# Later additions to x in both ffn_out stages, and three small edits in the attention of a macaron block on one core

## The chip, the core and the metric

The kernel runs on one core of a Trainium2 chip. A core has a matrix engine (TensorE, PE in the profile), a vector engine (VectorE, DVE), a scalar engine (ScalarE, ACT), a general engine (GpSimd, POOL) and a queue engine that issues most transfers (SyncE, SP). Each engine works through its own list of instructions in order; they meet only at semaphores. An instruction that must wait therefore holds up all that stand behind it on its engine, whatever these need.

The metric is the device time of one launch in microseconds (us), the median of several executions.

## The reference

One block: half a SwiGLU feed-forward, a causal mixer, and another half feed-forward. The depth is one, so the mixer is the stick-breaking attention. x has 1024 rows and 1024 columns, the feed-forward is 2816 wide, and there are 16 heads of 64.

```python
x = x + 0.5 * swiglu(rms_norm(x, g1), w1_in, w1_out)
x = x + stick_breaking_attention(rms_norm(x, gm), w_qkv, gq, gk, w_o)
x = x + 0.5 * swiglu(rms_norm(x, g2), w2_in, w2_out)

def swiglu(xn, w_in, w_out):
    gate, up = split(xn @ w_in, 2)
    return (silu(gate) * up) @ w_out

# stick breaking, for each head, t the later frame, s < t:
z = q[t] . k[s] / sqrt(64)            # q, k after rms_norm with gains
A[t, s] = sigmoid(z[t, s]) * prod over s < j < t of (1 - sigmoid(z[t, j]))
o[t] = sum over s of A[t, s] * v[s];  out = o @ w_o
```

Everything is float32.

## The kernel before

**Precision.** Each operand of a large matmul is kept as two parts, hi and lo, in the fast float format (fp32r). `split` makes them: ACT copies the number into the format (hi, L182), and DVE or POOL subtracts that from the number (lo, L183). `mm3` (L272) then issues three matmuls for each pair of tiles: hi by hi (L279), hi by lo of the weights (L280), lo by hi (L281).

**Order of the stages.** Feed-forward 1 (`first_pair`, `ffn_in`, `ffn_out`), attention with its output projection, feed-forward 2 (the same three functions). So `ffn_out` runs twice: as the first stage spoken of below, with `w1_out`, and as the last stage of the kernel, with `w2_out`.

**`ffn_out`.** The product h @ w_out is made by a Strassen-like scheme of seven products over halves, in the order of the table `SEVEN`: 5, 1, 4, 3, 7, 2, 6. Products accumulate in four PSUM banks each (`ma` or `mb`, one for every block of 128 rows, t = 0 to 3). Each product runs over six chunks of the inner dimension: chunks 0 to 4 with two steps of 128, chunk 5 with one. `operands` (L520) prepares a chunk: the sum of two weight tiles on DVE where the product needs one (L524), then hi of the weights on ACT and their lo on POOL, hi of h on ACT and its lo on DVE, or on POOL for the chunks in `ON_POOL_H` (1, 3 and 5 of product 6). In a trace `rp<-raw` is a part of the weights and `rp<-rh` one of h. The rooms for these parts hold four chunks and are used in turn.

When a product is complete, `result` (L566) adds its banks, times plus or minus one half, to x in SBUF, with one instruction on DVE for each block and half (L570). Product 2 goes to two places, so it has eight such additions. Product 6, the last one, does chunks 0 to 2 for all four blocks, and then chunks 3, 4, 5 block by block, so that each block's addition can follow at once.

**`held`.** Without it, product 2's eight additions are issued as soon as product 2 ends. With `held=n` the scale of these additions is not a constant but a tile, `signs`, which is first written from the lo part of h of chunk n of product 6 (L576) and then set to the constants (L536). The numbers are the same, but the additions can't come ahead of that lo part in DVE's list. Before the change the first stage has `held=2`; the last stage has none.

**What follows the additions in the first stage.** `at` (L665) hangs the work for the attention's input on them: squares of x on ACT (L217), the row norms on DVE (L242 writes the normalised rows, `xs`), stores of x to DRAM on SP (L672). The first weights of the attention come on the same queue (L733), are made hi on ACT (L739) and lo on POOL (L742), as wqh and wql.

**Attention.** Eight head pairs, in an interleaved plan. `weights_of` (L718) puts tiny writes, "holds", into the room of the next weights, so that ACT can't make these weights ahead of a given point: L738 writes 128x2 elements made from a given tile, on POOL or on DVE. `scores` (L829) makes a piece of w: two sigmoids on ACT (L853), a running product on DVE (L855, om), and their product on POOL (L862). `values` (L866) turns w by a transpose on PE (L884), splits it (th on ACT, tl on DVE), and multiplies with v (L902). `out_weights` (L1027) loads and splits w_o for the projection while the last pairs still run; its rooms are wa, wb, wc and so on.

Of the kernel before, what the change touches and what calls it, by code (L numbers as in the profile page):

```python
# [9 lines left out]
F32 = mybir.dt.float32  # L10
# [3 lines left out]
ALU = mybir.AluOpType  # L14
# [3 lines left out]
P = 128  # L18
# [88 lines left out]
def macaron_kernel(ctx, tc, x, g1, w1_in, w1_out, gm, w_qkv, gq, gk, w_o, g2, w2_in, w2_out, out):  # L107
# [64 lines left out]
    make_identity(nc, ident)  # L172
    xh = cpool.tile([P, KD, T], F32R, name="xh")
    xl = cpool.tile([P, KD, T], F32R, name="xl")
    above = cpool.tile([P, 96], F32, name="above")
    pool_e.memset(below, 0.0)
    pool_e.memset(above, 0.0)
    x_keep = [dram.tile([T, D], F32, name=f"x_keep{i}") for i in range(2)]
# [439 lines left out]
    with pools(*RAWS) as pr:  # L618
        ops = {}
        right = ExitStack()  # L620
        tl = mixed(right.enter_context(pools(*MIXED, side="right")))
        with banks("ps1"), pools(*STREAM) as pa:
            with pools("x") as px, pools("xs", "hs", side="right") as pl:
                rows_of = {}

                def load_x(tbs):
                    for tb in tbs:
                        rows_of[tb] = px["x"].tile([P, D], F32, name="x", bufs=NT)
                        sp.dma_start(rows_of[tb], x[rows(tb), :])

                def normed(tbs):
                    pending.extend(norm(pl, lambda tb, h: rows_of[tb][:, HALVES[h]], tbs, gain))

                def turn_rows(tbs):
                    while pending:
                        pending.pop(0)("kb", tl)
                    if tbs:
                        normed(tbs)

                load_x(ORDER[:2])  # L640
                gain = load_gain(pl, g1)
                ahead = [stream(pr, w1_in, 0, 0)]
                load_x(ORDER[2:4])
                ahead.append(stream(pr, w1_in, 0, 1))
                load_x(ORDER[4:])
                for tb in ORDER[:2]:
                    normed((tb,))

                us = first_weights(pa | pr, ahead, pending[1].args[0][:, D - 1 :])
                turn_rows(ORDER[2:4])  # L650
                at = {(0, 3): 4, (1, 1): 6, (2, 1): 8}
                hb = first_pair(
                    pa | pr, us, {w: lambda i=i: turn_rows(ORDER[i : i + 2]) for w, i in at.items()}
                )
            with pools(*SPLIT) as pt:
                ffn_in(pa | pr | pt, w1_in, keep, tl, hb, right, lambda: early(pr, w1_out, keep, ops))
        late = []
        norms = ExitStack()
        pn = norms.enter_context(pools("xs", "hs", side="right"))
        with banks("ps2"), pools(*SECOND) as pl:  # L660
            lay_banks()
            gain_m = load_gain(pn, gm)
            half = pn["xs"].tile([P, 4, 2], F32, name="half", bufs=1)

            def at(x_sb, m, where, ops):  # L665
                def row(tb, h):
                    return x_sb[h][:, tb, :]

                def store(tbs, hs):
                    for tb in tbs:  # L670
                        for h in hs:
                            sp.dma_start(x_keep[0][rows(tb), HALVES[h]], row(tb, h))  # L672

                def turn_rows(bk, n):
                    for _ in range(n):
                        pending.pop(0)(bk)

                if (m, where) == (7, "end"):
                    pending.extend(norm(pn, row, (4, 5), gain_m))
                    store((4, 5, 6, 7), (0, 1))  # L680
                elif (m, where) == (2, 2):
                    turn_rows("ma", 2)
                elif (m, where) == (2, 3):
                    late.append(rates(pn, row, (6, 7)))
                elif (m, where) == (6, 0):

                    there = ops[2][1][1][:, 0, 0:1].bitcast(F32)
                    pending.extend(norm(pn, row, (6, 7), gain_m, r=late.pop(), behind=there))
                elif (m, where) == (2, "end"):
                    squares(pn, row, range(4), half, (0,))  # L690
                    store(range(4), (0,))
                elif m == 6 and str(where).startswith("block"):
                    t = int(where[-1])
                    turn_rows("mb", (2, 0, 0, 1)[t])
                    squares(pn, row, (t,), half[:, t : t + 1], (1,))
                    late.append(lambda: pending.extend(norm(pn, row, (t,), gain_m, half[:, t : t + 1])))
                    if t < 3:
                        late.pop()()
                    store((t,), (1,))

            ffn_out(pl | pr, w1_out, keep, x, ops, at, held=2)

    on_banks = ExitStack()
    on_banks.enter_context(banks("psa"))
# [3 lines left out]
    with ExitStack() as stack:  # L708
# [9 lines left out]
        def weights_of(p, state, behind):  # L718

            wh, wl = state["wq"] = {}, {}

            def step(n, k):
                if k % 4 == 0:
                    wq = pl[f"wq{(2 * p + k // 4) % 4}"]
                    state["h"], state["l"] = (wq.tile([P, 4, 3 * P], F32R, name=f"wq{n}", bufs=1) for n in "hl")
                h_, l_ = state["h"], state["l"]
                raw = pl["raw_qkv"].tile([P, 2, 3, P], F32, name="raw_qkv")  # L730
                src = w_qkv[k * P : (k + 2) * P, :].rearrange("(k p) (a c) -> p k a c", p=P, a=3)
                for i in range(2):
                    sp.dma_start(raw[:, i], src[:, i, :, p * P : (p + 1) * P])  # L733
                ks = slice(k % 4, k % 4 + 2)
                raw = raw.rearrange("p k a c -> p k (a c)")
                for engine, to, f in behind[n]:
                    there = f().to_broadcast([P, 2])
                    engine.tensor_tensor((h_, l_)[to][:, ks, 0], there, there, op=ALU.mult)  # L738
                act.activation(h_[:, ks], raw, AF.Copy)  # L739
                for i in range(2):  # L740
                    k_ = k % 4 + i
                    pool_e.tensor_tensor(l_[:, k_, :], raw[:, i, :], h_[:, k_, :].bitcast(F32), op=ALU.subtract)  # L742
                    wh[k + i], wl[k + i] = h_[:, k % 4 + i, :], l_[:, k % 4 + i, :]

            return [partial(step, i // 2, k) for i, k in enumerate((4, 6, 0, 2) if p == 0 else (0, 2, 4, 6))]
# [83 lines left out]
        def scores(state, hd, half):  # L829
# [3 lines left out]
            def step(tb, kb):  # L833
                L = T - tb * P
                if kb == half:
                    t = pl["w"].tile([P, T - tb % 4 * P], F32, name=f"w{hd}{tb % 4}", bufs=1)

                    om = t[:, L : 2 * L] if half else pl["om"].tile([P, T], F32, name="om")
                    state["om"], w[tb] = om, t[:, :L]
                om, wt = state["om"], w[tb]  # L840
                q = state["q", hd, half][:, (tb % 4) * P : (tb % 4 + 1) * P]
                s0 = max(tb * P, kb * NHALF)
                n = (kb + 1) * NHALF - s0
                c0 = s0 - tb * P
                off = P if n == P else 0
                z = bank("bz")
                keys = slice(s0 - off - kb * NHALF, NHALF)
                for i in range(2):
                    pe.matmul(z[:, : off + n], q, state["k", hd, kb][i][:, keys], start=i == 0, stop=i == 1)  # L849

                z = z[:, off : off + n]
                for to, sign in ((wt[:, c0 : c0 + n], 0), (z, 1)):
                    act.activation(to, z, AF.Sigmoid, scale=state["f", half][:, sign, tb % 4, hd : hd + 1])  # L853
                least = first[:, P : P + 1].to_broadcast([P, n]) if c0 else first[:, :n]
                dve.tensor_tensor_scan(  # L855
                    om[:, c0 : c0 + n], z, least, initial=om[:, c0 - 1 : c0] if c0 else 0.0,
                    op0=ALU.mult, op1=ALU.max,
                )
                if c0 == 0:
                    pool_e.memset(wt[:, 0:1], 0.0)  # L860
                c1 = max(c0, 1)
                pool_e.tensor_tensor(wt[:, c1 : c0 + n], wt[:, c1 : c0 + n], om[:, c1 - 1 : c0 + n - 1], op=ALU.mult)  # L862

            return [partial(step, tb, kb) for tb in range(half * 4, half * 4 + 4) for kb in range(half, 2)]

# [157 lines left out]
    with pools(*PROJECTION) as pl:  # L1023
# [3 lines left out]
        def out_weights(c, k, rooms):  # L1027
# [7 lines left out]
            if c is HALVES[0] and k < 6:  # L1035

                there = seen[:, k // 2 : k // 2 + 1] if k < 4 else wo[-1][1][:, 0:1].bitcast(F32)
                pool_e.tensor_tensor((l_ if k < 4 else h_)[:, 0:1], there, there, op=ALU.mult)
            split(raw, h_, l_, lane(f"wo{k // 2}") if c is HALVES[0] else dve)
            return [(h_[:, s], l_[:, s]) for s in HALVES]  # L1040

        def project(tb, ks, h, tags):
# [48 lines left out]
    with banks("ps4"), pools(*SECOND) as pl:  # L1091
# [11 lines left out]
                for h in hs:  # L1103
                    sp.dma_start(out[rows(tb), HALVES[h]], x_sb[h][:, tb, :])

        ffn_out(pl | pr, w2_out, keep, x_keep[1], ops, at)
    after.close()


# [37 lines left out]
```

## Time and profile before

| | us |
|---|---|
| median of 3 runs | 1952.72 |
| lowest, highest | 1952.14, 1958.2 |
| the profiled execution | 1957.07 |
| span of its trace | 1955.3 |
| POOL busy | 1089.5 |
| DVE busy | 1265.6 |

The profile is one execution. A row of a timeline gives the start and the length of an instruction in us, its engine, its line in the program, the operation, and what it writes and reads (out<-in); in brackets stands how long the engine was idle before it, and what ended that. A list of waits gives, for an engine, which line waited for which line of which engine: total, times, longest. The chain that ended last is followed back from the last instruction of the kernel. A granted clock of 1.00 is TensorE's full speed.

### The profile page before, as it was taken

To read this page: it belongs to the slowest core of one execution; us is meant where nothing else is said; L and a number is where in the kernel's file an instruction comes from. 1 tells how busy PE (TensorE), PEld (TensorE's weight loads), DVE (VectorE), ACT (ScalarE), POOL (GpSimd) and SP (SyncE) were. 2 spreads that over 40 slices of the span, in tenths; PEclk is the share of its full clock that TensorE was granted. 3 is DMA by queue.
4 is the path that set the end of the run, shared out by engine and by line. 5 is a ranking of instruction groups with operands and counts; after the bars stand their busy time and mean duration, and the time that the engine had idled before them with its cause. 6 is when DMAs were issued, how large, how long until landed. Compare 5 with 4: busy or idle time off the path is not lost. (4 is left out here: it accounts for less than half of the span.)

```text
span 1955.3 us, 27335 instructions
## 1 busy us (share of the span) xinstructions
PE 1910.4 (98%) x9656; PEld 1638.2 (84%) x9656; DVE 1265.6 (65%) x1839; ACT 986.2 (50%) x1802; POOL 1089.5 (56%) x963
## 2 busy tenths in 40 slices
PE   7999999999999899999999999999999999999998
PEld 7978888888888798898989897789888888888886
DVE  7855545535766957877787878475555545557644
ACT  6533433434335467877787777344433443434331
POOL 3667666656455446555655664114667667655554
PEclk9999999999999999999999999999999999999999
DMA  6223223338996311011111144511323223369973
GB/s 210 85 88 126 101 92 114 107 113 284 343 325 231 124 34 44 31 46 45 36 34 46 55 130 151 194 55 44 130 86 124 96 99 105 117 231 345 325 251 128
DMA packets 168505, 260.26 MB, mean 133 GB/s; under 512 B 11568, under 2 KB 81200, under 8 KB 168368
## 3 DMA queue, kind: packets, MB, share of 16 engines
q1 hardware_dynamic: 168368, 258.52, 38.7%
q8 instruction: 75, 1.23, 0.3%
q14 instruction: 62, 0.51, 0.1%
HBM read 198.18 MB, written 60.29 MB: 132 GB/s over the span
## 5 line engine op out<-in xcount | busy, mean ns | idle before, releaser
L183 POOL TENSOR_TENSOR rp<-raw,rp 128x1024 fp32r<-128x1024 f32 x84 | 209.4, 2498 | 190.6 <-ACT rp L182 172.8
L183 POOL TENSOR_TENSOR u<-sf,u 128x512 fp32r<-128x512 f32 x160 | 225.9, 1414 | 151.1 <-ACT u L182 147.2
L183 POOL TENSOR_TENSOR u<-raw,u 128x512 fp32r<-128x512 f32 x136 | 195.8, 1444 | 164.7 <-ACT u L182 163.5
L182 ACT ACTIVATE u<-sf 128x512 fp32r<-128x512 f32 x160 | 100.7, 630 | 215.1 <-PE kb L280 86.7
L862 POOL TENSOR_TENSOR w<-w,om 128x512 f32<-128x512 f32 (+4 forms) x128 | 140.9, 1105 | 115.0 <-DVE om L855 88.8
L398 DVE TENSOR_TENSOR h<-h 128x512 f32<-128x512 f32 x110 | 135.4, 1235 | 85.7 <-POOL h L502 85.0
L279 PE MATMUL bq<-wqh,xh 128*128 128x384 f32 x512 | 174.7, 341 | 1.9 <-DVE vst L776 1.9
L182 ACT ACTIVATE rp<-rh 128x1024 fp32r<-128x1024 f32 (+1 forms) x78 | 76.4, 984 | 190.9 <-PE mb L280 62.0
L281 PE MATMUL bq<-wqh,xl 128*128 128x384 f32 x512 | 172.2, 336 | 0.0
L280 PE MATMUL bq<-wql,xh 128*128 128x384 f32 x512 | 172.1, 336 | 0.0
L279 PE MATMUL ka<-xh,u 128*128 128x512 f32 (+1 forms) x448 | 162.1, 362 | 1.8 <-ACT s L450 1.5
L280 PE MATMUL ka<-xl,u 128*128 128x512 f32 (+1 forms) x448 | 161.8, 361 | 0.0
L281 PE MATMUL ka<-xh,u 128*128 128x512 f32 (+1 forms) x448 | 161.6, 361 | 0.0
L182 ACT ACTIVATE u<-raw 128x512 fp32r<-128x512 f32 x136 | 85.0, 632 | 149.4 <-PE ka L280 101.3
L524 DVE TENSOR_TENSOR raw<-raw 128x1024 f32<-128x1024 f32 (+1 forms) x60 | 94.0, 1569 | 98.2 <-DMA raw<-w_out 92.4
L280 PE MATMUL ma<-rp 128*128 128x512 f32 x352 | 137.7, 391 | 4.4 <-POOL rp L183 4.4
L281 PE MATMUL ma<-rp 128*128 128x512 f32 x352 | 137.9, 392 | 3.3 <-DVE rp L183 3.3
L279 PE MATMUL ma<-rp 128*128 128x512 f32 x352 | 137.7, 391 | 0.0
L853 ACT ACTIVATE w<-bz,f 128x512 f32<-128x512 f32 (+2 forms) x192 | 112.3, 585 | 40.5 <-PE bz L849 39.4
L502 POOL TENSOR_TENSOR h<-h,g 128x512 f32<-128x512 f32 x80 | 112.9, 1411 | 35.2 <-DVE h L454 33.4
L427 DVE TENSOR_TENSOR sf<-raw 128x512 f32<-128x512 f32 x80 | 81.2, 1015 | 78.0 <-POOL u L183 78.0
L183 DVE TENSOR_TENSOR rp<-rh,rp 128x1024 fp32r<-128x1024 f32 (+1 forms) x70 | 108.4, 1567 | 22.4 <-ACT rp L182 19.7
(276 smaller groups left out, 5552.7 us busy)
## 6 DMA issues: line engine op xcount, KB each, us to landing
raw<-w_out SPq DMA_DIRECT2D x120, 512.0 KB, 5.6
raw<-w_in SPq DMA_DIRECT2D x88, 512.0 KB, 3.6
k<-h SPq DMA_DIRECT2D x154, 256.0 KB, 2.1
rh<-k SPq DMA_DIRECT2D x64, 512.0 KB, 6.2
raw_qkv<-w_qkv SPq DMA_DIRECT2D x64, 192.0 KB, 2.9
x_keep<-x SPq DMA_DIRECT2D x32, 256.0 KB, 3.5
x<-x_keep SPq DMA_DIRECT2D x32, 256.0 KB, 5.3
raw<-w_out SPq DMA_DIRECT2D x24, 256.0 KB, 4.3
```

Source lines behind the costliest of these rows:

```text
L182: act.activation(hi, raw, AF.Copy)
L183: (engine or dve).tensor_tensor(lo, raw, hi.bitcast(F32), op=ALU.subtract)
L279: pe.matmul(dst, ah, bh, start=start and i == 0, stop=False, skip_group_check=onto)
L280: pe.matmul(dst, ah, bl, start=False, stop=False, skip_group_check=onto)
L281: pe.matmul(dst, al, bh, start=False, stop=stop and i == n - 1, skip_group_check=onto)
L398: dve.tensor_tensor(src, hb[of[0]], hb[of[1]], op=getattr(ALU, of[2]))
L427: dve.tensor_tensor(f[n], x, y, op=op)
L502: pool_e.tensor_tensor(h, h, gs[k], op=ALU.mult)
L524: dve.tensor_tensor(w[0], w[0], w[1], op=getattr(ALU, W_OF[m][2]))
L853: act.activation(to, z, AF.Sigmoid, scale=state["f", half][:, sign, tb % 4, hd : hd + 1])
L862: pool_e.tensor_tensor(wt[:, c1 : c0 + n], wt[:, c1 : c0 + n], om[:, c1 - 1 : c0 + n - 1], op=ALU.mult)
```

## The change

Four edits. First, both calls of `ffn_out` pass `held=4`: the first stage had 2, the last stage none. `above`, a scratch tile, gives up eight columns for the second `signs` tile. Second, the holds on DVE (L738) are a TENSOR_SCALAR of one source rather than a TENSOR_TENSOR of the same source twice; their places stay. Third, the very last piece of w is multiplied on DVE and not on POOL. Fourth, in `out_weights` the lo part of one pair of weight tiles (k = 6 of the first half, wc on DVE) is written in two pieces of 128x512.

```diff
-    above = cpool.tile([P, 96], F32, name="above")
+    above = cpool.tile([P, 88], F32, name="above")
...
-            ffn_out(pl | pr, w1_out, keep, x, ops, at, held=2)
+            ffn_out(pl | pr, w1_out, keep, x, ops, at, held=4)
...
                     there = f().to_broadcast([P, 2])
-                    engine.tensor_tensor((h_, l_)[to][:, ks, 0], there, there, op=ALU.mult)
+                    if engine is dve:
+                        dve.tensor_scalar((h_, l_)[to][:, ks, 0], there, 1.0, None, op0=ALU.mult)
+                    else:
+                        engine.tensor_tensor((h_, l_)[to][:, ks, 0], there, there, op=ALU.mult)
...
-                pool_e.tensor_tensor(wt[:, c1 : c0 + n], wt[:, c1 : c0 + n], om[:, c1 - 1 : c0 + n - 1], op=ALU.mult)
+
+                last = state is states[NP - 1] and (hd, half, tb, kb) == (1, 0, 3, 1)
+                by = dve if last else pool_e
+                by.tensor_tensor(wt[:, c1 : c0 + n], wt[:, c1 : c0 + n], om[:, c1 - 1 : c0 + n - 1], op=ALU.mult)
...
-            split(raw, h_, l_, lane(f"wo{k // 2}") if c is HALVES[0] else dve)
+
+            act.activation(h_, raw, AF.Copy)
+            by = lane(f"wo{k // 2}") if c is HALVES[0] else dve
+            for s in HALVES if (c, k) == (HALVES[0], 6) else (slice(0, D),):
+                by.tensor_tensor(l_[:, s], raw[:, s], h_[:, s].bitcast(F32), op=ALU.subtract)
...
-        ffn_out(pl | pr, w2_out, keep, x_keep[1], ops, at)
+        ffn_out(pl | pr, w2_out, keep, x_keep[1], ops, at, held=4)
```

The order on the engines is set by a scheduler from the program, so `held` moves more than the additions. DVE in the first stage, from the addition of the weights of chunks 3 and 4 of product 6 (the first row) to the first addition to x (the last row), as a difference:

```order
 L524 TENSOR_TENSOR raw<-raw 128x1024 x2
 L183 TENSOR_TENSOR rp<-rh,rp 128x1024
+L240 TENSOR_SCALAR xs<-rp 128x1 x2
+L242 SCALAR_TENSOR_TENSOR xs<-x_4341,rs_y,gain 128x512
+L242 SCALAR_TENSOR_TENSOR xs<-x_4340,rs_y,gain 128x512 x2
+L524 TENSOR_TENSOR raw<-raw 128x512
+L183 TENSOR_TENSOR rp<-rh,rp 128x1024
 L576 TENSOR_SCALAR signs<-rp 128x2
-L240 TENSOR_SCALAR xs<-rp 128x1 x2
 L536 MEMSET signs 128x1 x2
-L242 SCALAR_TENSOR_TENSOR xs<-x_4340,rs_y,gain 128x512
 L570 SCALAR_TENSOR_TENSOR x_4340<-mb_5525,signs,x_4340 128x512
```

The two L183 are the lo parts of h of chunk 2 and chunk 4. Ahead of the additions there now stand three L242, the sum of chunk 5's weights (L524) and the lo part of chunk 4, which were among or behind the additions before; the eight additions are now together, with nothing between them.

ACT at the same place, before and then with the change, from chunk 3's parts to the hi part of the first weights of the attention. `rp` are parts of product 6, and `hs,half` are the squares, each of which waits for an addition to x:

```order
L182 ACTIVATE rp<-rh 128x1024
L182 ACTIVATE rp<-raw 128x1024
L217 ACTIVATE hs,half<-x_4340 128x512 x2
L182 ACTIVATE rp<-rh 128x1024
L182 ACTIVATE rp<-raw 128x1024
L217 ACTIVATE hs,half<-x_4340 128x512 x2
L182 ACTIVATE rp<-rh 128x512
L182 ACTIVATE rp<-raw 128x512
L739 ACTIVATE wqh<-raw_qkv 128x768 x2
```

```order
L182 ACTIVATE rp<-rh 128x1024
L182 ACTIVATE rp<-raw 128x1024
L182 ACTIVATE rp<-rh 128x1024
L182 ACTIVATE rp<-raw 128x1024
L217 ACTIVATE hs,half<-x_4340 128x512 x2
L182 ACTIVATE rp<-rh 128x512
L182 ACTIVATE rp<-raw 128x512
L217 ACTIVATE hs,half<-x_4340 128x512
L742 ACTIVATE wqh<-raw_qkv 128x768
L217 ACTIVATE hs,half<-x_4340 128x512
L742 ACTIVATE wqh<-raw_qkv 128x768
```

Chunk 4's two hi parts moved ahead of all squares; chunk 5's (128x512) stand behind two squares rather than four. (L742 of the changed kernel is L739 of the one before.)

DVE in the last stage, before (from the last two additions of product 2 to the first of product 6) and then with the change (from the sums of the weights of chunks 3 and 4 to the first two additions of product 2):

```order
L570 SCALAR_TENSOR_TENSOR x_17887<-mb_19044,x_17887 128x512
L570 SCALAR_TENSOR_TENSOR x_17888<-mb_19044,x_17888 128x512
L183 TENSOR_TENSOR rp<-rh,rp 128x1024
L524 TENSOR_TENSOR raw<-raw 128x512
L183 TENSOR_TENSOR rp<-rh,rp 128x1024
L570 SCALAR_TENSOR_TENSOR x_17888<-ma_19261,x_17888 128x512
```

```order
L524 TENSOR_TENSOR raw<-raw 128x1024 x2
L183 TENSOR_TENSOR rp<-rh,rp 128x1024
L524 TENSOR_TENSOR raw<-raw 128x512
L183 TENSOR_TENSOR rp<-rh,rp 128x1024
L576 TENSOR_SCALAR signs<-rp 128x2
L536 MEMSET signs 128x1 x2
L570 SCALAR_TENSOR_TENSOR x_17888<-mb_19042,signs,x_17888 128x512
L570 SCALAR_TENSOR_TENSOR x_17889<-mb_19042,signs,x_17889 128x512
```

The eight additions went from ahead of the two lo parts (chunk 2, chunk 4) and of the sum of chunk 5's weights to behind them.

Of the other lists: on SP in the first stage there were four stores of x and then eight loads of the attention's weights; now load and store alternate four times, a load first, and four loads follow. In the last stage the first store to the output moved behind the last load of w2_out. On PE one transpose (the w that DVE now makes) moved behind four other instructions. On DVE that multiply stands behind L908 and ahead of the next tl; the two pieces of wc follow each other at once.

## The prediction

> **What bounds the kernel now.** I read the page first, then PE's list of waits, then the chain of work that ended last, then the timeline at the places where these point.
>
> ```profile
> PE 1910.4 (98%) x9656; PEld 1638.2 (84%) x9656; DVE 1265.6 (65%) x1839; ACT 986.2 (50%) x1802; POOL 1089.5 (56%) x963
> ```
>
> PE is busy for 98% of the span of 1955.3 us, and the change takes no matmul away. So only time in which PE stands still, or runs below its pace, can be won. The list of PE's waits (total, times, longest) says where:
>
> ```profile
> PE bo L902 <- DVE tl L183: 7.7, 14, 1.2
> PE bt L884 <- POOL w L860: 4.7, 8, 0.6
> PE ma L280 <- POOL rp L183: 4.4, 2, 2.7
> PE ma L281 <- DVE rp L183: 3.3, 1, 3.3
> ```
>
> The last two rows are the sixth product of the two ffn_out stages, the place that `held` touches: twice in the first stage (4.4 us), once in the last one (3.3 us). The first row is spread over the attention. The chain that ended last comes out of the last stage:
>
> ```profile
> 1925.69 3.56 DVE x L570 x6
> ...
> 1929.80 1.22 DVE rp L183
> ...
> 1951.56 0.69 DVE x L570
> ```
>
> PE's end hangs there on one subtraction on DVE, the lo part of the h of chunk 2 (hl below), and that stands behind additions to x.
>
> **The last stage** (`held` from none to 4). First PE's timeline there, and from the table by windows the row behind the wait (length; busy time of PE, PEld, DVE, ACT, POOL; then the granted clock):
>
> ```profile
> 1927.15 0.39 PE L279 MATMUL ma<-rp 128*128 128x512 f32 x1
> 1927.38 0.39 PE L280 MATMUL ma<-rp 128*128 128x512 f32 x1
> 1931.06 0.79 PE L281 MATMUL ma<-rp 128*128 128x512 f32 x1 [3.30 <-DVE rp L183]
> ...
> 1934.82 0.39 PE L281 MATMUL ma<-rp 128*128 128x512 f32 x1
> 1931.00:1934.90 3.90, 3.84 (x10) 3.10 (x11) 1.75 (x3) 0.63 (x1) 1.47 (x1) 0.56 0.00 0
> ```
>
> PE's normal pace is 0.23 a step (1927.15 to 1927.38). From 1927.38 to 1934.82 there are 10 steps in 7.44 us, where 2.3 would do. So 5.1 us are lost: 3.4 by the wait, and 1.7 because the clock stood at 0.56 in the next 3.9 us (0.44 x 3.9). Now DVE and POOL:
>
> ```profile
> 1925.01 4.86 DVE L570 SCALAR_TENSOR_TENSOR x<-mb,x 128x512 f32<-128x512 f32 x8
> ...
> 1930.93 0.68 DVE L524 TENSOR_TENSOR raw<-raw 128x512 f32<-128x512 f32 x1
> 1931.53 1.21 DVE L183 TENSOR_TENSOR rp<-rh,rp 128x1024 fp32r<-128x1024 f32 x1
> 1926.32 2.38 POOL L183 TENSOR_TENSOR rp<-raw,rp 128x1024 fp32r<-128x1024 f32 x1 [2.31 <-ACT rp L182]
> ```
>
> After the change hl of chunk 2 starts at 1925.1, where the eight additions (4.86) started, and with its 1.21 is done by 1926.3; PE wants it at 1927.6. The addition of chunk 5's weights (0.68) and hl of chunk 4 (1.21) follow. A POOL subtraction beside them can stretch both (the same shape takes 3.42 at 643.01, below), so hl of chunk 4 ends between 1928.2 and 1931.2. PE wants it when the 24 steps of chunk 2 and seven more are done, at 1927.15 + 31 x 0.23 = 1934.3. The lo part of chunk 5's weights needs ACT and some 1.5 us of POOL behind the 0.68, so it is there by 1932.7 at the latest; PE wants it four to five steps later than hl of chunk 4. Then come `signs`, two memsets and the eight additions, done by about 1937. Block 0's addition waits behind them, which costs nothing: the one that ends the kernel is at 1951.56. On SP the first store to `out` goes behind the last load, and no one waits for it. Term: **-5.1 us**. If an execution has the wait without the slow clock, it is -3.4.
>
> Of such a clock the Trainium skill says ("TensorE: Matmul & The Clock Gate", Part 1) that an idle window of about 3.4 us halves it, that this window runs freely, and that the count of slow matmuls varies between runs. The trace agrees on the rate (the row of 0.56); whether other executions have it no row shows, and by that rule the term may lie at either of the two values above.
>
> **The first stage** (`held` from 2 to 4). PE, then ACT, DVE and POOL, which stand in each other's way:
>
> ```profile
> 656.10 0.50 PE L280 MATMUL ma<-rp 128*128 128x512 f32 x1 [2.69 <-POOL rp L183]
> ...
> 659.47 0.50 PE L280 MATMUL ma<-rp 128*128 128x512 f32 x1 [1.72 <-POOL rp L183]
> 641.50 1.06 ACT L182 ACTIVATE rp<-raw 128x1024 fp32r<-128x1024 f32 x1 [5.12 <-DVE raw L524]
> 648.17 0.63 ACT L217 ACTIVATE hs<-x 128x512 f32<-128x512 f32 x1 [5.61 <-DVE x L570]
> 643.01 3.42 DVE L183 TENSOR_TENSOR rp<-rh,rp 128x1024 fp32r<-128x1024 f32 x1
> ...
> 646.73 0.75 DVE L242 SCALAR_TENSOR_TENSOR xs<-x,rs_y,gain 128x512 f32<-128x512 f32 x1
> 647.39 1.40 DVE L570 SCALAR_TENSOR_TENSOR x<-mb,signs,x 128x512 f32<-128x512 f32 x2
> 642.64 2.71 POOL L183 TENSOR_TENSOR rp<-raw,rp 128x1024 fp32r<-128x1024 f32 x1 [2.32 <-ACT rp L182]
> 652.85 3.19 POOL L183 TENSOR_TENSOR rp<-raw,rp 128x1024 fp32r<-128x1024 f32 x1 [7.50 <-ACT rp L182]
> 656.00 1.75 POOL L183 TENSOR_TENSOR rp<-rh,rp 128x512 fp32r<-128x512 f32 x1
> 657.71 1.71 POOL L183 TENSOR_TENSOR rp<-raw,rp 128x512 fp32r<-128x512 f32 x1
> ```
>
> PE waits 2.69 us for POOL's lo of chunk 4's weights and 1.72 for that of chunk 5. Both are late because ACT sat 5.61 us in front of a square (L217) that waits for an addition, with the hi parts of both chunks behind it. After the change chunk 4's two hi parts stand ahead of the squares: ACT does them from 642.6 to 644.7 (1.06 each), POOL its lo from 645.35 to about 648.5 (3.19), and PE, which wants it at 656.10 - 2.69 = 653.4, waits no more. Chunk 5's hi parts still stand behind two squares, which wait for additions 1 and 3, and those are now later. DVE does hl of chunk 2 until 646.4, three L242 of 0.66 to 0.75 which POOL blocks until 648.5 (to 650.6), L524 (0.68), hl of chunk 4 (1.21), `signs` and memsets (0.3); so the additions start at about 652.7. The third ends at 654.8 (0.7 each), its square at 655.5, ACT's two parts of 0.6 at 656.7, and POOL's hl and then lo of chunk 5, short of the 1.7 that they take under contention, at about 659.0. PE gets there at 653.4 + (659.47 - 1.72 - 656.10) = 655.1. So one wait of 3.9 takes the place of 4.41. Term: **-0.5 us**. If POOL does not block the three L242, all is 2.0 earlier and the term is -2.5; at most -4.4. On the other side, one wait of 3.9 is longer than the 3.30 behind which the clock was at 0.56. If the clock goes down here too, 1.7 us are paid: **+1.2**.
>
> **The hold on DVE** (L738, twelve instructions), a TENSOR_TENSOR of 128x2 that becomes a TENSOR_SCALAR. The group by form (min, median, max in ns), and a TENSOR_SCALAR of 128x2 with its source in SBUF that met a busy POOL:
>
> ```profile
> L738 DVE TENSOR_TENSOR wqh<-r x12: 147/496/862, 754.2 to 1085.0; 128x2 fp32r<-128x2 f32 x12
> 613.32 2.25 DVE L194 TENSOR_SCALAR rs_y<-rs_a 128x2 int32<-128x2 int32 x1
> 613.11 2.43 POOL L183 TENSOR_TENSOR rp<-raw,rp 128x1024 fp32r<-128x1024 f32 x1 [1.19 <-ACT rp L182]
> ```
>
> The first hold of each of six pairs takes some 0.85 us, beside a POOL that runs; the second takes 0.15. If the new form were not blocked, 0.7 us per pair would be won, and the tl behind it, for which PE's L902 waits, would come that much earlier: 6 x 0.7 = -4.2. But L194, of the new form and size, lasted just until POOL ended (613.11 + 2.43 = 615.54; 613.32 + 2.25 = 615.57). That is the nearest row, so the term is **0**, with -4.2 as one end of the range and nothing above, as both forms wait for the same POOL instruction.
>
> The Trainium skill bears on both forms ("SBUF — State Buffer", SBUF: two separate sides): an op with two inputs in SBUF and an op in a two-port mode both take the port pair shared with GpSimd for their whole length. It speaks against a gain here, and the row of L194 agrees.
>
> **The hold split in two.** The wc on DVE is now two pieces of 128x512, one right behind the other:
>
> ```profile
> 1173.18 2.60 DVE L183 TENSOR_TENSOR wc<-raw,wb 128x1024 fp32r<-128x1024 f32 x1 [0.76 <-ACT wb L182]
> ```
>
> It took 2.60 where the shape takes 1.21 alone (row at 1931.53), so POOL blocked it. Two pieces cost 2 x 0.68 - 1.21 = 0.15 more, and nothing comes between them, so what is behind them comes no earlier: **+0.1**, between 0.15 worse and 0.7 better, should the first piece slip in ahead of POOL.
>
> **The last w on DVE.** DVE, POOL and PE around it:
>
> ```profile
> 1231.56 0.66 DVE L908 TENSOR_TENSOR o<-bo,o 64x512 f32<-64x512 f32 x1
> 1231.72 1.26 POOL L862 TENSOR_TENSOR w<-w,om 128x512 f32<-128x512 f32 x1 [5.66 <-DVE om L855]
> 1233.04 0.33 PE L884 MATMUL bt<-ident,w 128*128 128x128 f32 x1 [1.20 <-POOL w L862]
> ```
>
> On DVE it runs behind L908, from 1232.2 for 0.68 (the size of the row at 1930.93), to 1232.85. The transpose that needs it has four PE instructions put ahead of it, worth 0.8 us, so PE wants it at 1233.04 - 1.20 + 0.8 = 1232.7. Of the 1.20 some 0.15 stays: **-1.1**, between -1.2 and -0.5 (were DVE 0.5 late). The next work on DVE, tl, needs this transpose itself, so it loses nothing.
>
> **Sum**: -5.1 - 0.5 + 0 + 0.1 - 1.1 = -6.6 us against the profiled execution, 1957.07 with its span of 1955.3. That execution is 4.35 above the median, 1952.72, and no row says where; I take the sum off the median: 1946.1.
>
> **The rivals.** (1) The clock goes down in the first stage (1.7 more), or it stays up in the last stage of most executions before (1.7 less to win): -4.9, 1947.8. For the first speaks that the joined wait is longer than 3.30; against it, that two waits of 4.41 in sum, 1.65 apart, left no mark on PE's pace. (2) The lighter hold is not blocked: -6.6 - 4.2 = -10.8, 1941.9. Against it stands L194; for it, only that L194 writes another type. (3) The additions of the first stage, now 5.3 us later (652.7 for 647.4), take the attention's first weights with them, since on SP the loads of these now stand between the stores that wait for additions:
>
> ```profile
> 668.61 2.49 POOL L742 TENSOR_TENSOR wql<-raw_qkv,wqh 128x384 fp32r<-128x384 f32 x2 [0.61 <-ACT wqh L739]
> 672.81 0.42 PE L279 MATMUL bq<-wqh,xh 128*128 128x384 f32 x1
> ```
>
> The weights are ready at 671.1 and wanted at 672.8: a cover of 1.7. A delay d of them makes PE stand for d - 1.7; with the clock down there and at the joined wait, 1.2 + d - 1.7 + 1.7 = 1.2 + d is lost against 6.1 won elsewhere. At d = 5.3 this gives +0.4, 1953.1; from d = 4.9 on the kernel is slower than before, and at d = 12, which takes a delay that adds up over the alternating stores and loads, by 7.1: 1959.8. Against it: the first load now goes ahead of all stores, and the weights are wanted as late as before.
>
> **How the numbers follow.** About 0.3% (5.9 us, so 1946.9) is what a measurement of this kernel can tell from no change. The forecast has 0.50, rival 1 0.30, rival 2 0.12, rival 3 0.06; the other 0.02 are gains swallowed later, near 1951. The forecast lies just beyond the bound, and I count four fifths of it as faster. Faster: 0.40 + 0.12 = 0.52. Slower by over 0.3%: the far half of rival 3, 0.03. Within: 0.45. The range takes in the forecast and rival 1 with both its halves and the last w at its bad end (-6.6 + 1.7 + 1.7 + 0.6 = -2.6, 1950.1), rounded up to 1950.5, and reaches down to rival 2 with the first stage 0.9 better: 1941.
>
> **What would show it.** In the last stage: no wait of PE for DVE's rp, and the clock at 1.00 there. In the first: one wait for rp, on chunk 5, near 3.9 us, and the clock behind it. L738's maximum stays near 0.86 (0.15 by rival 2). No wait for w near 1232. Wrong would be: a wait for wql at the attention's start, L902's sum far below 7.7, or a new wait of PE in the last 30 us.

## The result, and the profile after

| | us |
|---|---|
| changed kernel, median of 4 | 1966.28 (1965.8 to 1967.04) |
| kernel before, median of 4 | 1953.1 (1952.14 to 1958.2) |
| ratio, with its 95% interval | 1.0063 (1.0045 to 1.008) |
| span of the trace, changed and before | 1964.6 and 1955.3 |

The changed kernel is slower by 13 us. 1946.1 was predicted, with a range to 1950.5. The page of the changed kernel, its row on busy time:

```profile
PE 1926.5 (98%) x9656; PEld 1636.3 (83%) x9656; DVE 1258.9 (64%) x1844; ACT 987.4 (50%) x1802; POOL 1092.1 (56%) x962
```

The same 9656 matmuls keep PE busy for 16.1 us longer (1926.5 for 1910.4). So the loss is no wait. The list of PE's waits confirms it; what the prediction spoke of went as it said:

```profile
PE bo L908 <- DVE tl L183: 7.2, 14, 1.0
...
PE ma L279 <- ACT rp L182: 1.7, 1, 1.7
PE ma L280 <- POOL rp L183: 1.6, 1, 1.6
...
PE bt L890 <- DVE w L868: 0.2, 1, 0.2
```

The wait of 3.3 us for DVE's rp in the last stage is gone, the two waits of 4.4 in the first stage became one place with 3.3 (first for ACT, then for POOL, both on chunk 5), the wait of 1.2 for the last w became 0.2, and L908 (L902 before) waits for tl as it did.

To find where the time went, I matched the two traces matmul by matmul (both have 9656, in nearly one order) and followed the difference of the starts. It grows by 6.9 us from 153 to 470 us, evenly, some 1.05 us for every 200 matmuls; it is 0.8 lower by 1390, with a swing of under 3 at the waits of the first stage; it grows again by 8.0 from 1390 to 1752, just as evenly; then 5.2 are won back in the last stage. The two stretches are `ffn_in` of the two feed-forwards, which no row of the change touches. The table by windows, of the changed kernel (length; busy time and count of PE, PEld, DVE, ACT, POOL; granted clock; the rest is DMA):

```profile
200.00:440.00 240.00, 240.00 (x1036) 194.10 (x1035) 113.97 (x125) 93.88 (x161) 153.94 (x110) 1.00 0.30 100
500.00:640.00 140.00, 139.99 (x625) 115.68 (x624) 94.45 (x102) 58.81 (x75) 72.52 (x30) 1.00 0.83 298
1400.00:1700.00 300.00, 300.00 (x1296) 242.66 (x1295) 148.36 (x161) 118.63 (x202) 194.50 (x139) 1.00 0.31 103
```

and of the kernel before:

```profile
200.00:440.00 240.00, 240.00 (x1060) 198.73 (x1059) 118.83 (x126) 94.81 (x163) 153.12 (x110) 1.00 0.31 106
500.00:640.00 140.00, 140.00 (x626) 115.86 (x625) 96.34 (x104) 59.49 (x75) 74.60 (x30) 1.00 0.84 296
1400.00:1700.00 300.00, 300.00 (x1325) 248.42 (x1324) 156.20 (x165) 119.54 (x206) 198.40 (x143) 1.00 0.30 102
```

In `ffn_in` (first and third row) PE is busy all the time in both kernels and at full clock in both, but does 1036 matmuls in 240 us where it did 1060: 0.2317 us a step for 0.2264. In `ffn_out` (second row) nothing changed. The rows by form of one of the three matmuls in that window, first changed, then before, show where the growth appears:

```profile
L280 PEld LDWEIGHTS ka<-xl,u x100: 187/187/188, 202.1 to 438.0; 128*128 128x128 f32 x100
L280 PE MATMUL ka<-xl,u x100: 393/394/397, 202.4 to 438.2; 128*128 128x512 f32 x100
```

```profile
L280 PEld LDWEIGHTS ka<-xl,u x104: 187/188/188, 200.7 to 436.7; 128*128 128x128 f32 x104
L280 PE MATMUL ka<-xl,u x104: 389/389/389, 200.9 to 436.9; 128*128 128x512 f32 x104
```

The load of the weights (u, 128x128) takes 188 ns as before; the matmul that streams xl takes 394 for 389, and is no longer the same each time. (The profile models the ends of matmuls, so the pace from start to start is the measure, not this length.)

What the change did to `ffn_in` is its first line, the one that looked like bookkeeping: `above` from 96 to 88 columns. That tile is filled with zeros and never read. It is a pad: the tiles allocated behind it lie where they lie because of its size. In the built programs (bytes from the start of a partition):

```
tile              before    changed
xh                  2752       2752     the x operand, streamed
u (the first)     126144     126112     the weights of ffn_in
t0h               146624     146592     sums of x, streamed too
rp (the first)    146624     146592     operands of ffn_out
signs, 1st/2nd     68672      68640, both
```

Most tiles moved down by 32 bytes; xh and xl, which lie ahead of `above`, did not, nor did those at the other end of SBUF, such as sf, g, s and xs of `ffn_in`. The room was not needed either: the two `signs` tiles share one address, since the pool gives a second tile of the same name the place of the first.

### The profile page after: what moved, and what is told of

It reads as the page before. It is cut to its first block, busy times and chain, and to the rows that moved or that the text cites. A ratio compares the mean times of both kernels' runs of the same rounds, so it can differ in the third digit from the quotient of the medians.

```text
span 1964.6 us, 27340 instructions
## 1 busy us (share of the span) xinstructions
PE 1926.5 (98%) x9656; PEld 1636.3 (83%) x9656; DVE 1258.9 (64%) x1844; ACT 987.4 (50%) x1802; POOL 1092.1 (56%) x962
## 4 chain that ended last, share of the span: by engine, by line
PE 82%; DVE 9%; ACT 3%; issue 3%; DMA 2%; POOL 2%; SPq 0%; DVEq 0%; ACTq 0%; POOLq 0%
PE ka L279 6%; PE ka L281 6%; PE ka L280 6%; PE kc L279 4%; PE kc L281 4%; PE kc L280 4%; PE kb L279 4%; PE kb L281 4%; PE kb L280 4%; PE ma L280 3%; PE ma L279 3%; PE ma L281 3%; PE bq L279 3%; PE bq L281 3%; PE bq L280 3%; PE bo L908 3%
## 5 line engine op out<-in xcount | busy, mean ns | idle before, releaser
L183 POOL TENSOR_TENSOR rp<-raw,rp 128x1024 fp32r<-128x1024 f32 x84 | 210.9, 2516 | 179.9 <-ACT rp L182 167.2
L183 POOL TENSOR_TENSOR u<-sf,u 128x512 fp32r<-128x512 f32 x160 | 231.3, 1447 | 139.1 <-ACT u L182 137.4
L183 POOL TENSOR_TENSOR u<-raw,u 128x512 fp32r<-128x512 f32 x136 | 192.3, 1419 | 196.7 <-ACT u L182 196.2
L182 ACT ACTIVATE u<-sf 128x512 fp32r<-128x512 f32 x160 | 101.0, 632 | 226.7 <-PE kb L280 91.3
L868 POOL TENSOR_TENSOR w<-w,om 128x511 f32<-128x511 f32 (+3 forms) x127 | 139.8, 1104 | 109.2 <-DVE om L858 83.0
L524 DVE TENSOR_TENSOR raw<-raw 128x1024 f32<-128x1024 f32 (+1 forms) x60 | 91.5, 1527 | 96.8 <-DMA raw<-w_out 94.9
L183 DVE TENSOR_TENSOR rp<-rh,rp 128x1024 fp32r<-128x1024 f32 (+1 forms) x70 | 113.4, 1638 | 22.5 <-ACT rp L182 19.7
```

Source lines behind the costliest of these rows:

```text
L182: act.activation(hi, raw, AF.Copy)
L183: (engine or dve).tensor_tensor(lo, raw, hi.bitcast(F32), op=ALU.subtract)
L524: dve.tensor_tensor(w[0], w[0], w[1], op=getattr(ALU, W_OF[m][2]))
L868: by.tensor_tensor(wt[:, c1 : c0 + n], wt[:, c1 : c0 + n], om[:, c1 - 1 : c0 + n - 1], op=ALU.mult)
```

## The experiments

**Undo the pad; make the pad alone.** Two theories stand against each other.

```diff
# e1: the changed kernel
-    above = cpool.tile([P, 88], F32, name="above")
+    above = cpool.tile([P, 96], F32, name="above")
# e2: the kernel before
-    above = cpool.tile([P, 96], F32, name="above")
+    above = cpool.tile([P, 88], F32, name="above")
```

> The changed kernel with `above` at 96 columns again, so that every tile lies where it lay before the change. Theory A (the 32 bytes by which the smaller `above` moves nearly all tiles slow TensorE in both ffn_in stages): the 14.4 us of the two ffn_in stages come back, 1966.3 - 14.4 = about 1952, the pace there is 0.227 us a step as before, and the other edits keep what they won. Theory B (the later additions or the other edits make the loss): still about 1966.

Measured: 1951.13 (1950.35 to 1952.19, 12 runs), beside 1956.46 of the kernel before in the same job; ratio 0.9977 (0.9966 to 0.9987). The pace in `ffn_in` is the old one (1060 matmuls from 200 to 440 us).

> The kernel before with `above` at 88 columns and nothing else changed. Theory A: slower by about 14 us, near 1967, with a pace of 0.232 us a step in both ffn_in stages and the old waits of PE near 653, 1231 and 1927 us still there. Theory B: no change, 1953.

Measured: 1971.36 (1966.88 to 1976.52, 6 runs), ratio 1.0078 (1.0057 to 1.0099); 1037 matmuls from 200 to 440 us; the old waits are all there. So theory A holds from both sides: eight columns of a tile that no one reads cost some 15 us (1971.36 - 1956.46 here, 1966.28 - 1951.13 in the changed kernel), and without them the rest of the change is a gain. Theory B falls.

**What about the place matters.** Four runs moved tiles by other steps, by the sizes of `above` and of `below`, a pad ahead of ident and xh.

```diff
# e3: the changed kernel, all behind xl 64 bytes lower than before the change
+    above = cpool.tile([P, 80], F32, name="above")
# e4: the kernel before, xh and all behind it 32 bytes lower
+    below = cpool.tile([P, 8], F32, name="below")
# e6: the kernel before, ident, xh and xl alone 32 bytes lower
+    below = cpool.tile([P, 8], F32, name="below")
+    above = cpool.tile([P, 104], F32, name="above")
# e7, e8: the kernel before, all behind xl 128 and 256 bytes lower
+    above = cpool.tile([P, 64], F32, name="above")    # e7
+    above = cpool.tile([P, 32], F32, name="above")    # e8
```

> The changed kernel with `above` at 80 columns: everything lies 64 bytes lower than before the change, not 32. Theory A1 (what counts is whether tiles start on a multiple of 64 bytes): the old pace, 0.227, and the time of the run with 96 columns, about 1952. Theory A2 (any shift of u against xh slows it, or the place of before is special): a pace of 0.23 or more, and 1960 to 1967.

> The kernel before with the tile ahead of xh (`below`) at 8 columns: ident, xh, xl and all that follows lie 32 bytes lower, so u and xh are both 32 bytes off a multiple of 64. Theory A1a (weights that start off a multiple of 64 load more slowly, whatever the other operand): a pace of 0.232 or more in the ffn_in stages, 1967. Theory A1b (it is u against the moving operand, one on 64 bytes and the other 32 off): a pace of 0.227 to 0.230, 1953 to 1960.

> The kernel before with `below` at 8 and `above` at 104 columns: ident, xh and xl alone lie 32 bytes lower, u and all the rest where they lay. Theory A1b (the place of u against the moving operand decides): slow ffn_in steps with xh (0.228 to 0.235 us), though u has its old place; some 1960 to 1972. Theory A1a' (the place of u and of the tiles above it decides, or their distance from the tiles of the other end of SBUF): the old pace 0.227, 1953 to 1957.

> The kernel before with `above` at 64 columns: u lies 128 bytes lower against xh. If what counts is the distance modulo 128, the pace is 0.227 (1953 to 1957); if modulo 256, 512 or more, it is above 0.227 in the ffn_in steps with xh, less than the 0.2335 of 32 bytes if the price falls with the distance, as from 32 to 64 (0.2299).

> The kernel before with `above` at 32 columns: u lies 256 bytes lower against xh. Modulo 256: the pace 0.227. Modulo 512 or more: above 0.227.

Measured. The pace is the mean from start to start of consecutive matmuls in `ffn_in` (200 to 440 and 1400 to 1700 us), worked out from the traces, apart for steps that stream xh or xl, and those that stream t0, t1 or t3; the distance is the start of u less that of xh, modulo 256. The tiles t move with u, so theirs is 0 in each run.

| run | distance u - xh | ns a step with xh, xl | with t | time, us |
|---|---|---|---|---|
| before | 0 | 226.7 | 226.7 | 1957.07 |
| e4 (both 32 lower) | 0 | 226.7 | 226.7 | 1957.22 |
| e8 (u 256 lower) | 0 | 226.7 | 226.7 | 1957.43 |
| e2 (u 32 lower) | 224 | 233.6 | 229.7 | 1971.36 |
| changed (u 32 lower) | 224 | 233.5 | 229.8 | 1966.28 |
| e6 (xh 32 lower) | 32 | 233.5 | 228.7 | 1970.66 |
| e7 (u 128 lower) | 128 | 232.8 | 227.9 | 1964.65 |
| e3 (u 64 lower) | 192 | 229.9 | 230.8 | 1962.58 |

(Of before, e4, e6, e7 and e8 the time is that of one execution; of the others the median. The times differ by more than the pace: the profiles of before, e2, e4, e6 and e8 have the wait of 3.3 us in the last stage, that of e7 one of 0.5, those of the changed kernel and e3 none. So the pace is what to compare.)

Each run struck out a theory. e3: a multiple of 64 bytes is not enough (1962.58, not 1952). e4: it is not that u starts off a multiple of 64, for there it does and the pace is the old one. This is its row of the table by windows:

```profile
200.00:440.00 240.00, 240.00 (x1061) 198.72 (x1060) 118.83 (x126) 95.43 (x164) 155.21 (x110) 1.00 0.31 106
```

e6: u has its old place, and only xh moved, and yet it is slow; so neither is it the place of u, nor its distance to the tiles that ACT, DVE and POOL use. Its row:

```profile
200.00:440.00 240.00, 240.00 (x1039) 194.76 (x1038) 114.19 (x125) 94.19 (x160) 152.52 (x110) 1.00 0.31 102
```

e7 and e8: 128 bytes are slow and 256 are not. What counts for the steps with xh, in all eight, is the distance between the weights and the streamed operand, modulo 256 bytes; distances other than these were not tried.

The steps with t, at distance 0, are slowed too. In the changed kernel the twelve steps of such a product take 241, 224, 231, 236, 228, 233, 231, 226, 227, 227, 226, 227 ns: late at first, then at the old pace. They always follow a product with xh, and in each of the five slow runs they are back at 227 by the eleventh step at the latest (in e3, where they are slower on average than the steps with xh, it takes that long). So this looks like a lag carried over from the product before; that is argued from the order, not tried. The expectation that the price falls as the distance grows fell: 128 costs more than 64.

**The last stage alone**, and **the first stage undone**.

```diff
# e9: the kernel before
-        ffn_out(pl | pr, w2_out, keep, x_keep[1], ops, at)
+        ffn_out(pl | pr, w2_out, keep, x_keep[1], ops, at, held=4)
# e10: e1 with
-            ffn_out(pl | pr, w1_out, keep, x, ops, at, held=4)
+            ffn_out(pl | pr, w1_out, keep, x, ops, at, held=2)
```

> The kernel before with `held=4` in the last stage alone (one edit of the change; every tile where it was before). By the prediction's term for the last stage: the wait of PE for DVE's rp near 1927 goes, 5.1 us less where an execution before had that wait with the slow clock, 3.4 where it had it without, less where it had a shorter wait (the run with 64 columns had 0.5): in the median 3 to 5 us below the kernel before. Rival (the eight additions behind the lo parts delay the last block): no gain.

Measured: 1952.27 (1951.41 to 1953.25, 12 runs) beside 1956.66; ratio 0.9984 (0.9974 to 0.9993). The difference of the medians, 4.4, lies in the expected 3 to 5; but the times of the kernel before fall into two groups (below, at e12), and e9 is as fast as the faster of them.

> The changed kernel with `above` at 96 and the first stage back at `held=2`: all of the change but its edit of the first stage. If the first stage's edit is worth what the trace of the run with 96 columns shows (waits of 3.7 with a slow clock for waits of 4.4, then a wait near 683 us that is gone: within 0.5 us of nothing), this is the same time as that run, 1.5 to 2 us above the run with `held=5`. By the prediction's term it is 0.5 us slower than the run with 96 columns; if the slow clock costs all of 1.7, it is 1.2 faster.

Measured: 1952.24 (1950.45 to 1953.72, 12 runs), ratio 0.9985 (0.9976 to 0.9995), where e1 had 0.9977 (0.9966 to 0.9987): by the times, the edit of the first stage can't be told from nothing. The expectation took it that only the joined wait of e1 brings the slow clock. The trace of e10 has it with the two separate waits too (2.6 and 1.4 us). The rows of e1 and then of e10 (the clock is the number after the five engines):

```profile
640.00:690.00 50.00, 46.16 (x224) 40.29 (x223) 41.41 (x93) 20.29 (x41) 22.64 (x23) 0.93 0.32 105
640.00:690.00 50.00, 45.32 (x221) 39.25 (x220) 41.91 (x93) 20.57 (x41) 22.73 (x23) 0.93 0.32 102
```

The kernel before had 1.00 there. By the difference of the starts from 640 to 693 us, e10 loses 1.1 us against the kernel before and e1 0.5. So at an equally low clock the edit gains 0.6, near the 0.5 of the prediction; that is one execution of each.

**The kernel before once more.** Of its 23 times in the job of e9 and e10, ten lie between 1951.16 and 1953.17 (and none of 12 in e9 lies above 1953.25), and thirteen from 1956.53 on. The median of the ten is 1952.3, that of e9 1952.27.

> The kernel before once more, unchanged, for a second profile. Its times so far fall into two groups, 1951 to 1954 and 1956 to 1960. If the difference is the wait of PE for DVE's rp in the last stage with the slow clock behind it, an execution near 1952 has a wait there below 1 us and one near 1957 has 3.3 us with a clock near 0.56. If the difference lies elsewhere, the wait is there whatever the time.

Measured: 1951.46, and its list of waits has no row for DVE's rp. DVE there:

```profile
1917.13 1.59 DVE L524 TENSOR_TENSOR raw<-raw 128x1024 f32<-128x1024 f32 x1 [2.50 <-DMA raw<-w_out]
1918.65 4.86 DVE L570 SCALAR_TENSOR_TENSOR x<-mb,x 128x512 f32<-128x512 f32 x8
1923.43 3.44 DVE L183 TENSOR_TENSOR rp<-rh,rp 128x1024 fp32r<-128x1024 f32 x1
```

The same eight additions in the same order, but they started at 1918.65, not 1925.01: the sum ahead of them was through earlier, and hl of chunk 2 was done at 1926.9, in time. In the first profile that sum was this row:

```profile
1921.73 3.36 DVE L524 TENSOR_TENSOR raw<-raw 128x1024 f32<-128x1024 f32 x1 [2.34 <-POOL rp L183]
```

Matched matmul by matmul, the two profiles lie within some 0.5 us of each other up to 1927 us, and 5.6 apart from 1935 on. So the wait of the last stage, with the clock behind it, is what makes the one execution 5 us longer than the other. That all executions of the two groups divide in this way is inferred from their times, and from e9, which takes the wait away and has no time in the slower group. Why the sum is through earlier in some executions stays open.

**Chunk 5 ahead of all squares.** What the trace of e1 shows of the first stage, PE's timeline at the wait:

```profile
657.09 0.49 PE L279 MATMUL ma<-rp 128*128 128x512 f32 x1 [2.13 <-ACT rp L182]
659.16 0.79 PE L280 MATMUL ma<-rp 128*128 128x512 f32 x1 [1.57 <-POOL rp L183]
```

and its table by windows right behind them:

```profile
659.20:662.60 3.40, 3.40 (x14) 3.10 (x15) 0.89 (x2) 1.93 (x5) 2.58 (x3) 0.50 0.45 153
662.60:668.00 5.40, 5.40 (x23) 4.58 (x22) 4.96 (x13) 3.24 (x7) 3.29 (x6) 0.77 0.64 192
```

One wait of 3.7 in two pieces, and behind it a clock of 0.50 for 3.4 us and 0.77 in the next 5.4 (1.7 + 1.2 us lost). With `held=5` ACT's list has chunk 5's hi parts ahead of the squares.

```diff
# e5: e1 with
-            ffn_out(pl | pr, w1_out, keep, x, ops, at, held=4)
+            ffn_out(pl | pr, w1_out, keep, x, ops, at, held=5)
```

> The changed kernel with `above` at 96 and, in the first stage, `held=5`: the additions then wait for the lo part of h of chunk 5, and on ACT the hi parts of chunk 5 stand ahead of all squares, the only move. Theory C (the joined wait of the first stage is ACT's, standing in front of squares): POOL has chunk 5's weights by about 654, ahead of PE's want at 655, so the wait of 3.7 us and the slow clock behind it (1.7) go, 1 to 1.5 us of that come back as a wait near 683, and the time is 3.5 to 4.5 us below the run with 96 columns. Rival (the later squares and stores put the attention's first weights or rows late): a new wait between 665 and 700 us takes it all, no gain or a loss.

Measured: 1949.65 (9 runs) beside 1953.68; ratio 0.9972 (0.9962 to 0.9982); span 1947.5 for 1949.5. The waits for rp are gone, but only 2.0 us of the 3.5 to 4.5 came by the spans, 1.5 by the medians of the two jobs. The rest went into a new wait, in PE's list, and a slow clock that came back in part, 0.97 over 50 us (second row) where e1 had 0.93:

```profile
PE mb L254 <- DVE x L570: 2.3, 4, 0.7
```

```profile
640.00:690.00 50.00, 47.37 (x236) 41.21 (x235) 42.94 (x93) 20.92 (x42) 23.16 (x23) 0.97 0.35 112
```

PE reaches the transposes of the next rows (L254) sooner, and they write the banks mb that the eight additions still read, one bank each 1.3 us. Theory C had neither this wait nor the clock behind it.

**A hold that POOL can't block.** In e1 the TENSOR_SCALAR of 128x2 is blocked like the TENSOR_TENSOR was, as its rows by form show:

```profile
L739 DVE TENSOR_SCALAR wqh<-r x12: 154/505/866, 755.3 to 1085.9; 128x2 fp32r<-128x2 f32 x12
```

But no TENSOR_SCALAR of 128x1 in the traces was. So each hold was written as two of one element.

```diff
# e11: e5 with
-                        dve.tensor_scalar((h_, l_)[to][:, ks, 0], there, 1.0, None, op0=ALU.mult)
+                        for k_ in range(ks.start, ks.stop):
+                            dve.tensor_scalar((h_, l_)[to][:, k_, 0:1], f(), 1.0, None, op0=ALU.mult)
```

> The run with `held=5`, and each hold on DVE as two TENSOR_SCALARs of 128x1 rather than one of 128x2. In the traces so far a TENSOR_SCALAR of 128x1 took 0.14 to 0.155 us beside a busy POOL, and one of 128x2 waited for POOL's end. If that holds here: four holds a pair of 0.15 us each, PE's waits in L908 for tl fall from 7.6 to 4 to 5 us, and the time is 2 to 3.5 us below the run with `held=5`. Rival (what is behind the hold waits for the same POOL instruction anyway, since tl has two inputs in SBUF or PSUM): no change.

Measured: 1946.28 (1945.35 to 1948.0, 6 runs) beside 1956.66; ratio 0.9953 (0.994 to 0.9966), the best version, faster than both kernels. It is 3.4 us below e5 by the medians of the two jobs and 2.8 by the spans, as expected. The holds by form, and PE's row for tl in the list of waits of e5 and then of e11:

```profile
L740 DVE TENSOR_SCALAR wqh<-r x24: 143/145/147, 753.7 to 1081.1; 128x1 fp32r<-128x1 f32 x24
```

```profile
PE bo L908 <- DVE tl L183: 7.6, 14, 0.9
...
PE bo L909 <- DVE tl L183: 3.0, 8, 1.0
```

The timeline of DVE and POOL in one pair:

```profile
753.73 0.27 DVE L740 TENSOR_SCALAR wqh<-r 128x1 fp32r<-128x1 f32 x3
753.91 0.68 DVE L183 TENSOR_TENSOR tl<-bt,th 128x512 fp32r<-128x512 f32 x1
...
753.27 1.29 POOL L869 TENSOR_TENSOR w<-w,om 128x512 f32<-128x512 f32 x1 [2.11 <-DVE rs_u L197]
```

POOL is busy from 753.27 to 754.56, and three holds pass in 0.27 us, where one hold took up to 0.866, until POOL ended. The tl behind them has one input in PSUM and one in SBUF, and it is not blocked either. PE's sum of waits falls from 7.6 to 3.0. The rival falls. (The fourth hold stands behind that tl in DVE's list, and delays nothing.)

## Why the prediction was wrong

**The step that failed** is its first: "the change takes no matmul away. So only time in which PE stands still, or runs below its pace, can be won". It looked for time to be won and took the pace of the matmuls that were not touched as fixed. The sum has five terms, and `above` is in none of them; I had read it as room for the second `signs` tile, and such it is described ahead of the prediction. It was the largest term: +6.9 and +8.0 in the two `ffn_in` (the growth of the difference of the starts, above), some +15 by e1 and e2. A resized tile that costs nothing by its instructions was still an edit of where everything lies: it moved the weights of `ffn_in` against the operand that streams past them, and the pace of 0.227 us a step became 0.232.

**The other terms**, by the trace of e1, which has all of the change but the pad:

| term | forecast | measured | from |
|---|---|---|---|
| last stage | -5.1 | -5.2 | difference of the starts, 1843 to 1951 us |
| first stage | -0.5 (+1.2 with the clock) | +0.5 with the clock (-0.6 against e10) | the same, 640 to 693 us |
| hold on DVE | 0 | 0 | 866 ns at most, for 862 |
| hold in two pieces | +0.1 | -0.2 | PE's step at that place, 1.42 us for 1.63 |
| last w | -1.1 | -1.0 | difference of the starts, 1230 to 1240 us |

Against the profiled execution of before the sum was -6.6, and the span of e1 is 5.8 lower (1949.5 for 1955.3). So these terms were right, and in the first stage the times behind them nearly so: the additions were forecast for 652.7 and came at 653.12, and the joined wait for 3.9 and came as 3.7. There rival 1, on the clock, came true, but not for its reason, since e10 has the slow clock without the joined wait. Its price differed from trace to trace: 2.9 us in e1 by the two windows, where the prediction had 1.7, but some 1.5 in the changed kernel, by its row:

```profile
640.00:690.00 50.00, 46.72 (x224) 39.62 (x223) 45.30 (x91) 20.13 (x36) 24.22 (x17) 0.97 0.42 137
```

The stage of e1 was 2.0 behind by 674 us; 1.5 of that went again between 674 and 686 us, 0.8 of it where PE had waited before anyway (its two waits for vst, 1.9 us, became one of 1.1).

**A second step was off**: "I take the sum off the median". Of the 6.6 us, 5.1 belong to a wait that the profiled execution had and that some executions don't have, as e12 shows. The three times on which the median rested were 1952.72, 1952.14 and 1958.2: by their size, two without it. I had noted that the profiled execution was 4.35 above the median and that no row says where; the wait was the place. Against executions without it the sum, pad aside, should have been -6.6 + 5.1 = -1.5. In e1's job ten of the 21 times of the kernel before lie below 1954, with a median of 1952.4; e1 is 1.3 below that. So even with the pad left alone the forecast of 1946.1 would have been 5 us too low: e1 took 1951.13.

**The rivals**: the one that ends slower (weights late, over the stores) did not happen; no wait for wql is in the list. That the lighter hold is not blocked is refuted for the 128x2 of the change, by e1, and true for 128x1, by e11, where it won some 3 us of the 4.2 at which the prediction priced it.

## What to carry to other kernels

Before you price a change by its instructions, compare where the tiles lie before and after it: a scratch tile that no one reads may be there to set the addresses, and a resized tile moves those that are laid out behind it. If PE is busy throughout, count its matmuls per window in both traces; a loss that is in no list of waits shows there at once. Ask whether a stall that you mean to remove is in all executions, by holding the profiled time against the others, before you take its price off the median.

## What the runs showed of the hardware

- **TensorE's pace depends on where its two operands lie to each other.** A 128x512 step in fp32r, with weights of 128x128, took 226.7 ns when the distance was 0 modulo 256 bytes (three layouts, those of before, e4 and e8), and 229.9 to 233.6 at a distance of 32, 128, 192 or 224 (four layouts), at a granted clock of 1.00. In the attention's qkv matmuls (128x384) the same shifts changed little: 174 to 176 ns, the median from start to start, at distances 0, 32, 128, 192 and 224. Of the mechanism the runs show only that it lies between the two operands, by e4 and e6. The Trainium skill says ("SBUF — State Buffer", SBUF: two separate sides) that PE waits for no other engine at that memory; these runs don't speak against it, and no run shows whether it is PE's own two reads that disturb each other. Whether `ffn_out` would slow down, whose operands always moved together here, was not tried.
- **The slow clock behind a wait is not sure.** In the last stage a wait of 3.3 us was followed by it in the kernel before, e2, e4 and e8 (0.56 to 0.66 over the next 3.9 us), and not in e6 (1.00), which lost 1.6 us less for it. In the first stage two waits of 2.0 to 2.7 and 1.4 to 1.7 us were followed by it in e2 and e10 (0.94 from 640 to 700 us and 0.93 from 640 to 690), and not in the kernel before, e4, e6, e7, e8 and e9 (1.00); the kernel before had it there in its second profile, e12 (0.97). The joined wait of the changed kernel, e1 and e3 was followed by it each time (0.97, 0.93, 0.97).
- **A hold of one element a partition was not blocked by POOL, one of two was.** As a TENSOR_SCALAR of 128x1 it took 0.143 to 0.147 us, 24 times in e11, 18 of them wholly inside a POOL instruction. Of 128x2, the first of each pair took 0.855 to 0.866 us in e1 and ended with the POOL instruction beside it.
